# Sampled tokens' output projection and second MLP product from unsplit fp32 operands in two column tiles, with another order of Strassen's products in that block

## The chip, the core and the metric

The kernel runs on one core of a Trainium2 chip. The metric is device time in microseconds of one execution. The engines are named as in the profile: PE (matrix products; PEld is its loading of stationary operands), DVE, ACT, POOL, and SP, which here issues most of the DMA loads.

## The reference

One inference step of a one-layer decoder trunk: 2048 prompt tokens and 64 sampled tokens (8 sequences of 8), width 1024, MLP width 4096, all in fp32. Attention with a forget gate and an mLSTM run beside each other; what concerns the change is the end of the layer, the same for prompt and sampled tokens:

```python
mix = concat([fox_h, mn]) @ w_o                       # output projection, 1024 x 1024
x1  = layer_norm(DN_ALPHA * x + mix, ln1_g, ln1_b)
hid = square(relu(x1 @ w1))                           # first MLP product, 1024 x 4096
y   = layer_norm(DN_ALPHA * x1 + hid @ w2, ln2_g, ln2_b)   # second MLP product, 4096 x 1024
```

## The kernel before

Tokens are cut into 17 tiles: 0 to 15 are 128 prompt tokens each, tile 16 is the 64 sampled tokens. The last phase, `phase_c`, computes the MLP in four blocks of four tiles; the last block (`ci == 3`) has tile 16 as well, so its width `W` is 576 columns instead of 512.

**fp32 through splits.** PE multiplies in fp32r, a faster form that keeps fewer bits. To keep fp32 precision, an operand is split into a high part (ACT copies it to fp32r, `split_hi`, L154) and a low part (DVE subtracts, `split_lo`, L157), and one product becomes three matmuls (`mm3`, L163 to L165). Weights go the same way: `raw()` takes a 512 KB buffer "wr" out of a ring of five (pool `pcw`), SP's queue loads it (in `piece`, L1114), and `piece` splits it into `wh` and `wl` (rings of four). In the kernel before, the raw weights are free again when both splits have read them.

**The MLP in groups.** The 4096 hidden units are done in 16 half-groups of 256: `hidden(p, half)` multiplies the block's tokens by a piece of w1 (two 512 KB loads), and ACT applies relu and square into `hq`. `output(p)` multiplies the hidden units of both halves of group p by w2 with Strassen's seven products in place of eight: for 512 tokens, 512 hidden units and 1024 columns. Each product is 12 matmuls of 512 columns (two token tiles, two steps of 128 hidden units, three of `mm3`) and takes one 512 KB weight: a quarter of w2 (products 1, 2, 3) or a sum of quarters that was prepared in DRAM (`dw2`; products 5, 6, 7, 4). `operands(p)` makes the sums of hidden units on DVE; `s` is the one buffer for them. `add` adds a result to the rows `y` on DVE (L1328), and takes the final norm (`norm_quick`) where a tile's last sum has come in. Products are made ready up to three places ahead (`order[:at_ + 3]`).

**Tile 16's share.** Strassen's products pair up 128-token tiles; tile 16 stands outside. Its hidden units times w2 are plain products, "extras" in the code, with the raw quarters of w2, which are those of products 1, 5, 3 and 2: six `mm3` matmuls of 512 columns with 64 tokens stationary behind each of these four products, from splits `hsh`, `hsl` of the hidden units. Results go to PSUM tile `ph`, and five adds of 64 x 512 go to `y`.

**The sampled stage.** Tile 16's output projection (`sampled`) runs between the two feature halves of `hidden(7, 1)` in block `ci == 2`: four column chunks of 256, each from two loads of w_o that are split; 96 matmuls of 256 columns in PSUM tile `py`. Then tile 16's first norm is taken and its rows go to DRAM, from where the last block takes them.

**Norm vectors.** `vecs(l)` loads the scale and offset of norm l, broadcast over the partitions, into two buffers of the same ring "wr". `C["gb"]` holds those of the second norm: they are loaded at `p == 7` of each block, in the last block ahead of the third product (`at_ == 2`).

**Order.** Each engine works its instructions in the order written into the program. That order is made when the program is built: a planner goes by its own estimates of when instructions are ready, and the code adds constraints (`issue_after`). So it need not be the order of the source. DMA queues start a load when its buffer is free; a load that waits holds up those behind it in the same queue.

Of the kernel before, what the change touches and what calls it, by code (L numbers as in the profile page):

```python
# [10 lines left out]
F32 = mybir.dt.float32  # L11
F32R = mybir.dt.float32r
I32 = mybir.dt.int32
AF = mybir.ActivationFunctionType
OP = mybir.AluOpType
# [21 lines left out]
ALPHA = 2.0 ** 0.25  # L37
# [15 lines left out]
def body(ctx, tc, I, O, stages):  # L53
# [99 lines left out]
    def split_hi(dst, src, scale=1.0):  # L153
        last["ACT"] = A.activation(dst, src, AF.Copy, scale=scale)  # L154

    def split_lo(dst, src, hi, eng=None):
        r = (eng or V).tensor_tensor(dst, src, hi.bitcast(F32), op=OP.subtract)  # L157
        if eng is None:
            last["DVE"] = r
        return r  # L160

    def mm3(ps, wh, wl, xh, xl, first, stop, shared=False):
        T.matmul(ps, wh, xh, start=first, stop=False, skip_group_check=shared)  # L163
        T.matmul(ps, wh, xl, start=False, stop=False, skip_group_check=shared)  # L164
        last["PE"] = T.matmul(ps, wl, xh, start=False, stop=stop, skip_group_check=shared)  # L165

    def layer_norm(x, np_, g, b, wk, tg, eng=None):
        st = wk.tile([128, 2, 6], F32, name="ln_st")
# [911 lines left out]
    def raw():  # L1080

        return pcw.tile([128, 1024], F32, name="wr", bufs=5)
# [165 lines left out]
    def phase_c():  # L1248
# [10 lines left out]
        def sampled():  # L1259

            gb = vecs(1)
            mx = ph.tile([128, 8, 64], F32, name="mxs", tag="s", bufs=1)
            SY.dma_start(mx, dmv[:, :, S:])
            mh = ph.tile([128, 8, 64], F32R, name="mhs", tag="hh", bufs=3)
            ml = ph.tile([128, 8, 64], F32R, name="mls", tag="hl", bufs=3)
            split_hi(mh, mx)
            split_lo(ml, mx, mh)
            y = row()
            SY.dma_start(y[:64], x_of(16))
            for c in range(4):  # L1270
                ps = ppc.tile([128, 512], F32, name="py", bufs=4)[:64, :256]
                for kg in range(2):
                    wh, wl = piece(wo[kg * 512:kg * 512 + 512, c * 256:c * 256 + 256].rearrange("(k p) c -> p k c", p=128))
                    for k in range(4):
                        mm3(ps, mh[:, kg * 4 + k], ml[:, kg * 4 + k], wh[:, k], wl[:, k], kg + k == 0, kg + k == 4)
                s = slice(c * 256, c * 256 + 256)
                V.scalar_tensor_tensor(y[:64, s], y[:64, s], ALPHA, ps, op0=OP.mult, op1=OP.add)
                if c == 0:
                    st = pc.tile([128, 2, 6], F32, name="ln_s2", bufs=5)
                if c % 2:  # L1280
                    V.bn_stats(st[:64, c // 2], y[:64, c * 256 - 256:c * 256 + 256])
            C["normed"] = norm_quick(y[:64], 64, st, *gb, pc, dx1[S:], SY)
# [11 lines left out]
        for ci, blk in enumerate(CB):  # L1294
# [45 lines left out]
            def operands(p):  # L1340

                f1, f2 = H.pop((p, 0)), H.pop((p, 1))
                a11, a21, a12, a22 = f1[:, :, 0:256], f1[:, :, 256:512], f2[:, :, 0:256], f2[:, :, 256:512]
                s = ph.tile([128, 2, 256], F32, name="s", bufs=1)

                def split(x):
                    h = ph.tile([128, 2, 256], F32R, name="hh", bufs=3)
                    l = ph.tile([128, 2, 256], F32R, name="hl", bufs=3)
                    split_hi(h, x)
                    split_lo(l, x, h)  # L1350
                    return h, l

                def w(src):
                    return piece(src.rearrange("p (k c) -> p k c", k=2))

                v = lambda o, x, y, op: V.tensor_tensor(o, x, y, op=op)

                def made(n):
                    if n == 1:
                        r = split(a11), w(I["w2"][p, 0])  # L1360
                        v(s, a21, a22, OP.subtract)
                        v(a21, a11, a21, OP.subtract)
                        v(a11, s, a11, OP.subtract)
                    elif n == 5:
                        r = split(s), w(dw2[p, 0])
                        v(s, a12, a11, OP.add)
                    else:
                        r = {6: lambda: (split(a11), w(dw2[p, 2])), 3: lambda: (split(s), w(I["w2"][p, 3])),
                             7: lambda: (split(a21), w(dw2[p, 1])), 2: lambda: (split(a12), w(I["w2"][p, 2])),
                             4: lambda: (split(a22), w(dw2[p, 3]))}[n]()  # L1370
                    return r

                hs = []
                if W > 512:
                    for f in (f1, f2):
                        x = f[:, :, 512:576]
                        h = ph.tile([128, 2, 64], F32R, name="hsh", bufs=2)
                        l = ph.tile([128, 2, 64], F32R, name="hsl", bufs=2)
                        split_hi(h, x)
                        split_lo(l, x, h)  # L1380
                        hs.append((h, l))
                return made, hs

            def output(p, ahead, begun=None):
                made, hs, ops = ahead
                if p == 0:
                    for t in blk:
                        ys[t] = row()
                        with tc.issue_after(last["ACT"].ins):
                            A.dma_start(ys[t][:tok_n(t)], dx1[tok_r(t):tok_r(t) + tok_n(t)])  # L1390
                X = [ppc.tile([128, 512], F32, name="py", bufs=4) for _ in range(2)]
                Z = None
                ADD, SUB = OP.add, OP.subtract
                plan = {1: ("X", True, False, 0, 0, ADD), 5: ("Z", True, False, 2, 1, ADD), 6: ("X", False, False, 0, 1, SUB),
                        3: ("Z", False, True, 0, 1, ADD), 7: ("X", False, False, 2, 1, SUB), 2: ("Y", True, True, 0, 0, ADD),
                        4: ("X", False, True, 2, 0, ADD)}
                extra = {1: (0, ((0, ADD), (1, SUB))), 5: (0, ((1, ADD),)), 3: (1, ((1, ADD),)), 2: (1, ((0, ADD),))}
                order = (1, 5, 6, 3, 2, 7, 4) if ci == 3 and p == 7 else (1, 5, 6, 3, 7, 2, 4)
                for at_, n in enumerate(order):
                    kind, first_, last_, r0, half, op = plan[n]  # L1400
                    if p == 7 and at_ == 2 and ci == 3:
                        C["gb"] = vecs(2)
                    for m in order[:at_ + 3]:
                        if m not in ops:
                            ops[m] = made(m)
                    (h, l), (wh, wl) = ops[n]
                    for i in range(2):
                        if kind == "X":
                            ps = X[i]
                        else:  # L1410
                            if i == 0 and first_:
                                Z = [None, None]
                            if first_:
                                Z[i] = ppc.tile([128, 512], F32, name="py", bufs=4)
                            ps = Z[i]
                        c = slice(i * 128, i * 128 + 128)
                        for k in range(2):
                            mm3(ps, h[:, k, c], l[:, k, c], wh[:, k], wl[:, k], first_ and k == 0, last_ and k == 1, True)
                        add(blk[r0 + i], half, ps, op)
                        tick(1.28)  # L1420
                        if begun and at_ < 4:
                            turn(ci + 1, at_, i, begun)
                    if n in extra and hs:
                        e, halves = extra[n]
                        ps = ppc.tile([128, 512], F32, name="ph", tag="ph", bufs=2)[:64]
                        for k in range(2):
                            mm3(ps, hs[e][0][:, k], hs[e][1][:, k], wh[:, k], wl[:, k], k == 0, k == 1)
                        for q, op in halves:
                            add(16, q, ps, op)
                        tick(1.28)  # L1430
                if begun:
                    for hf in range(2):
                        turn(ci + 1, 4, hf, begun)
# [19 lines left out]
            for p in range(8):  # L1453
                pre = []
                if p < 7:
                    hidden(p + 1, 0, lambda: pre.append(ahead(p, 1, 5)))
                else:
                    pre.append(ahead(p, 1))
                if p == 6:
# [451 lines left out]
```

## Time and profile before

| | |
|---|---|
| median of 3 runs | 3283.68 us (3271.96 to 3284.96) |
| profiled execution, its own time | 3288.64 us |
| its span in the profile | 3286.9 us |
| mean granted PE clock | 0.983 |
| PE busy | 3157.8 us, 96% |
| DVE, ACT, POOL busy | 64%, 46%, 28% |
| sampled stage | about 2816 to 2830 us of the span |
| last block | about 2860 us to the end |

Times in the profile are microseconds from the start of the span. A row of a timeline gives start, duration, engine, line, operation, tiles, and in brackets the idle time ahead of it with what ended that. A matmul's duration covers its whole way through the pipeline, so durations overlap, and the step from one start to the next tells what one costs. A row of windows gives the stretch, its length, the busy time of PE, PEld, DVE, ACT and POOL, the granted clock, the DMA share and GB/s.

### The profile page before, as it was taken

How to read it: one execution, taken by the hardware profiler on the slowest of the kernel's cores; microseconds unless marked ns; L12 is line 12 of the kernel's file. 1: busy time of each engine (PE TensorE's matmuls, PEld its weight loads, DVE VectorE, ACT ScalarE, POOL GpSimd, SP SyncE). 2: the span in 40 equal slices, each digit the busy share in tenths (PEclk: the TensorE clock that was granted, in tenths of full speed). 3: DMA queues.
4: the chain of work that ended last, by engine and by line, in shares of the span. 5: the costliest groups of instructions: out<-in, count | busy, mean ns of one | idle time of the engine just before them, and what ended most of it. 6: DMA issues, size and time to landing. Idle time of an engine off the chain costs nothing.

```text
span 3286.9 us, 58040 instructions
## 1 busy us (share of the span) xinstructions
PE 3157.8 (96%) x21681; PEld 2568.5 (78%) x21681; DVE 2099.3 (64%) x5083; ACT 1503.5 (46%) x2965; POOL 905.2 (28%) x974
## 2 busy tenths in 40 slices
PE   8999999898979999999999999999999999899997
PEld 8998998887856666677677777777777777798895
DVE  6957565355368787643466658656585666866658
ACT  3343343333358888622334444344454444444442
POOL 0121232322324333276323323333323121000000
PEclk9999999999989999999999999999999999999998
DMA  5575776766678675487887877878779766643332
GB/s 186 149 223 178 238 227 215 238 223 202 218 226 225 157 197 144 159 297 252 307 298 266 293 256 283 318 259 328 283 273 347 241 216 204 201 165 119 121 104 100
DMA packets 339777, 734.36 MB, mean 223 GB/s; under 512 B 63656, under 2 KB 177704, under 8 KB 338600
## 3 DMA queue, kind: packets, MB, share of 16 engines
q1 hardware_dynamic: 252936, 416.71, 39.8%
q0 software_dynamic: 83520, 304.12, 26.7%
q10 hardware_dynamic: 3040, 9.83, 0.8%
q8 instruction: 171, 2.80, 0.3%
q14 instruction: 110, 0.90, 0.1%
HBM read 677.71 MB, written 86.38 MB: 232 GB/s over the span
## 4 chain that ended last, share of the span: by engine, by line
PE 44%; DVE 3%; DMA 2%; issue 1%; POOL 1%; ACT 1%; another core or an unknown queue 0%; DVEq 0%; POOLq 0%
PE ph L163 7%; PE ph L164 7%; PE ph L165 7%; PE py L163 6%; PE py L165 6%; PE py L164 5%; PE sO L1767 2%; PE sQ L1655 2%; DMA vt<-cache_v,idxV 1%; DVE y L1328 1%; DVE wl L157 1%; DMA kT<-cache_k,idxK 1%; PE sT L1724 1%; POOL kT L1632 0%; DMA xr<-cache_v,idxV 0%
## 5 line engine op out<-in xcount | busy, mean ns | idle before, releaser
L157 DVE TENSOR_TENSOR wl<-wr,wh 128x1024 fp32r<-128x1024 f32 x364 | 443.8, 1222 | 364.3 <-ACT wh L154 338.0
L154 ACT ACTIVATE wh<-wr 128x1024 fp32r<-128x1024 f32 x364 | 383.0, 1055 | 320.0 <-PE ph L164 121.8
L163 PE MATMUL ph<-x1h,wh 128*128 128x512 f32 (+1 forms) x1280 | 454.8, 355 | 0.0
L1632 POOL DMA_INDIRECT kT<-cache_k,idxK x256 | 276.5, 1080 | 647.2 <-PE sQ L1655 580.1
L164 PE MATMUL ph<-x1l,wh 128*128 128x512 f32 (+1 forms) x1280 | 452.8, 354 | 0.2 <-DVE x1l L157 0.2
L165 PE MATMUL ph<-x1h,wl 128*128 128x512 f32 (+1 forms) x1280 | 450.2, 353 | 0.0
L163 PE MATMUL py<-wh,hh 128*128 128x512 f32 x896 | 358.0, 402 | 4.2 <-ACT hh L154 1.6
L164 PE MATMUL py<-wl,hh 128*128 128x512 f32 x896 | 353.3, 394 | 3.5 <-DVE wl L157 3.3
L165 PE MATMUL py<-wh,hl 128*128 128x512 f32 x896 | 350.5, 394 | 1.9 <-DVE hl L157 1.9
L1328 DVE TENSOR_TENSOR y<-y,py 128x512 f32<-128x512 f32 x416 | 281.0, 682 | 72.1 <-PE py L165 54.1
L163 PE MATMUL pm<-xh,whi 128*128 128x256 f32 (+1 forms) x1024 | 302.1, 295 | 1.1 <-issue 1.0
L164 PE MATMUL pm<-xl,whi 128*128 128x256 f32 (+1 forms) x1024 | 298.6, 292 | 2.9 <-issue 2.7
L165 PE MATMUL pm<-xh,wlo 128*128 128x256 f32 (+1 forms) x1024 | 297.1, 290 | 1.9 <-issue 1.8
L163 PEld LDWEIGHTS ph<-x1h,wh 128*128 128x128 f32 x1280 | 240.4, 188 | 41.2 <-issue 9.1
L1743 POOL DMA_INDIRECT vt<-cache_v,idxV x164 | 175.8, 1072 | 349.6 <-PE sO L1767 281.2
L164 PEld LDWEIGHTS ph<-x1l,wh 128*128 128x128 f32 x1280 | 240.5, 188 | 34.1 <-issue 3.7
L165 PEld LDWEIGHTS ph<-x1h,wl 128*128 128x128 f32 x1280 | 240.1, 188 | 33.7 <-issue 3.3
L163 PE MATMUL pm<-whi,xh 128*128 128x256 f32 (+2 forms) x816 | 238.7, 293 | 8.8 <-ACT whi L154 8.3
L164 PE MATMUL pm<-wlo,xh 128*128 128x256 f32 (+2 forms) x816 | 234.0, 287 | 1.3 <-issue 0.7
L165 PE MATMUL pm<-whi,xl 128*128 128x256 f32 (+2 forms) x816 | 233.7, 287 | 0.9 <-issue 0.9
L975 ACT ACTIVATE S<-S,mx 128x512 f32<-128x512 f32 (+2 forms) x320 | 208.6, 656 | 16.7 <-DVE mx L961 15.0
L163 PEld LDWEIGHTS py<-wh,hh 128*128 128x128 f32 x896 | 168.8, 189 | 54.3 <-issue 10.6
(372 smaller groups left out, 6821.8 us busy)
## 6 DMA issues: line engine op xcount, KB each, us to landing
wr<-w SPq DMA_DIRECT2D x224, 512.0 KB
wr<-dw SPq DMA_DIRECT2D x128, 512.0 KB
wra<-w_in SPq DMA_DIRECT2D x104, 512.0 KB
dw<-w POOLq DMA_DIRECT2D x48, 512.0 KB
Rb<-dR SPq DMA_DIRECT2D x128, 128.0 KB
xn<-xp_t SPq DMA_DIRECT2D x16, 512.0 KB
kn<-k_prompt SPq DMA_DIRECT2D x64, 128.0 KB
qn<-dq SPq DMA_DIRECT2D x128, 64.0 KB
```

Of the source, the lines that this page charges most:

```text
L154: last["ACT"] = A.activation(dst, src, AF.Copy, scale=scale)
L157: r = (eng or V).tensor_tensor(dst, src, hi.bitcast(F32), op=OP.subtract)
L163: T.matmul(ps, wh, xh, start=first, stop=False, skip_group_check=shared)
L164: T.matmul(ps, wh, xl, start=False, stop=False, skip_group_check=shared)
L165: last["PE"] = T.matmul(ps, wl, xh, start=False, stop=stop, skip_group_check=shared)
L975: last["ACT"] = A.activation(sp[:, :w], sp[:, :w], AF.Exp, bias=mx[:, 7:8], accum_out=lp[:, k:k + 1])
L1328: V.tensor_tensor(y, y, ps, op=op)
L1632: G.indirect_dma_start(out=piece(n), out_offset=None, in_=ck, in_offset=IO(ap=idxK[:, b, j // 2, j % 2:j % 2 + 1], axis=0))
L1655: r = T.matmul(pq[h4 * 32:h4 * 32 + 32, hg].rearrange("p (k c) -> p k c", k=2), z["qb"][:, hd], kv, start=(db == 0), stop=(db == 1), skip_ ...
L1724: T.transpose(p[:, f], z["U"][u][:, hg, f].rearrange("p k t -> p (k t)"), ident)
L1743: G.indirect_dma_start(out=vt.rearrange("p f c -> p (f c)"), out_offset=None, in_=cv, in_offset=IO(ap=idxV[:, b, (kt % 4) * 4 + kt // 4, f ...
L1767: after_ = T.matmul(po[r:r + 32], z["PT"][:, hg, 2 * f + g, pg].rearrange("p h q -> p (h q)"), vts[f][:, g, hg * 256:(hg + 1) * 256], star ...
```

## The change

A new helper, `two_sides`, multiplies unsplit fp32 operands: two products at a time, one into PSUM partitions 0 to 63, the other into partitions 64 to 127, that is, in two tiles of 64 columns of the PE array.

- In `sampled`, mixed activations and w_o stay unsplit. Each column chunk takes four pairs (one matmul on the first half of the contraction, one on the second), and the two halves of PSUM are added to `y` one after the other. The eight weight splits and the split of `mxs` go; raw weights are read by PE itself.
- In the last block, the products' order becomes 1, 2, 5, 3, 6, 7, 4. Tile 16's extras are taken twice per group: behind product 2 with the raw weights of products 1 and 2, behind product 3 with those of 5 and 3; four fp32 matmuls each. The splits `hsh`, `hsl` go. `w()` hands the raw tile on, so it is kept until the extra has read it.
- In the last group of the last block the norm vectors are loaded ahead of the fifth product (`at_ == 4`), no longer ahead of the third.

```diff
+    def two_sides(ps, sides, first, stop):
+
+        for n, (w, x) in enumerate(sides):
+            last["PE"] = T.matmul(ps[n * 64:n * 64 + 64], w, x, start=first, stop=stop, skip_group_check=True)
...
             mx = ph.tile([128, 8, 64], F32, name="mxs", tag="s", bufs=1)
             SY.dma_start(mx, dmv[:, :, S:])
-            mh = ph.tile([128, 8, 64], F32R, name="mhs", tag="hh", bufs=3)
-            ml = ph.tile([128, 8, 64], F32R, name="mls", tag="hl", bufs=3)
-            split_hi(mh, mx)
-            split_lo(ml, mx, mh)
...
-                ps = ppc.tile([128, 512], F32, name="py", bufs=4)[:64, :256]
+                ps = ppc.tile([128, 512], F32, name="py", bufs=4)[:, :256]
+                w = []
                 for kg in range(2):
-                    wh, wl = piece(wo[kg * 512:kg * 512 + 512, c * 256:c * 256 + 256].rearrange("(k p) c -> p k c", p=128))
-                    for k in range(4):
-                        mm3(ps, mh[:, kg * 4 + k], ml[:, kg * 4 + k], wh[:, k], wl[:, k], kg + k == 0, kg + k == 4)
+                    w.append(raw().rearrange("p (k c) -> p k c", k=4))
+                    SY.dma_start(w[kg], wo[kg * 512:kg * 512 + 512, c * 256:c * 256 + 256].rearrange("(k p) c -> p k c", p=128))
+                for k in range(4):
+                    two_sides(ps, [(mx[:, kg * 4 + k], w[kg][:, k]) for kg in range(2)], k == 0, k == 3)
                 s = slice(c * 256, c * 256 + 256)
-                V.scalar_tensor_tensor(y[:64, s], y[:64, s], ALPHA, ps, op0=OP.mult, op1=OP.add)
+                V.scalar_tensor_tensor(y[:64, s], y[:64, s], ALPHA, ps[:64], op0=OP.mult, op1=OP.add)
+                V.tensor_tensor(y[:64, s], y[:64, s], ps[64:128], op=OP.add)
...
                 def w(src):
-                    return piece(src.rearrange("p (k c) -> p k c", k=2))
+                    wr = raw().rearrange("p (k c) -> p k c", k=2)
+                    SY.dma_start(wr, src.rearrange("p (k c) -> p k c", k=2))
+                    return (*piece(None, wr), wr)
...
-                hs = []
-                if W > 512:
-                    for f in (f1, f2):
-                        x = f[:, :, 512:576]
-                        h = ph.tile([128, 2, 64], F32R, name="hsh", bufs=2)
-                        l = ph.tile([128, 2, 64], F32R, name="hsl", bufs=2)
-                        split_hi(h, x)
-                        split_lo(l, x, h)
-                        hs.append((h, l))
+                hs = [f[:, :, 512:576] for f in (f1, f2)] if W > 512 else []
                 return made, hs
+
+            order = (1, 2, 5, 3, 6, 7, 4) if W > 512 else (1, 5, 6, 3, 7, 2, 4)
...
-                extra = {1: (0, ((0, ADD), (1, SUB))), 5: (0, ((1, ADD),)), 3: (1, ((1, ADD),)), 2: (1, ((0, ADD),))}
-                order = (1, 5, 6, 3, 2, 7, 4) if ci == 3 and p == 7 else (1, 5, 6, 3, 7, 2, 4)
+                extra = {2: (1, ((0, 0, ADD), (0, 1, SUB), (1, 0, ADD))), 3: (5, ((0, 1, ADD), (1, 1, ADD)))}
                 for at_, n in enumerate(order):
                     kind, first_, last_, r0, half, op = plan[n]
-                    if p == 7 and at_ == 2 and ci == 3:
+                    if p == 7 and at_ == 4 and ci == 3:
                         C["gb"] = vecs(2)
...
-                    (h, l), (wh, wl) = ops[n]
+                    (h, l), (wh, wl, wr) = ops[n]
...
                     if n in extra and hs:
-                        e, halves = extra[n]
-                        ps = ppc.tile([128, 512], F32, name="ph", tag="ph", bufs=2)[:64]
+                        e, parts = extra[n]
+                        ps = ppc.tile([128, 512], F32, name="ph", tag="ph", bufs=2)
+                        w = ops[e][1][2], wr
                         for k in range(2):
-                            mm3(ps, hs[e][0][:, k], hs[e][1][:, k], wh[:, k], wl[:, k], k == 0, k == 1)
-                        for q, op in halves:
-                            add(16, q, ps, op)
+                            two_sides(ps, [(hs[i][:, k], w[i][:, k]) for i in range(2)], k == 0, k == 1)
+                        for i, q, op in parts:
+                            add(16, q, ps[i * 64:i * 64 + 64], op)
...
-                    hidden(p + 1, 0, lambda: pre.append(ahead(p, 1, 5)))
+                    hidden(p + 1, 0, lambda: pre.append(ahead(p, *order[:2])))
```

## The prediction

> **What bounds the kernel now.** I read the page first (the span, the engines, the chain that ended last), then the busy time by windows over the last 480 us, where the change lies, then the waits of PE and of SP's queue there, and last the records of single operations.
>
> ```profile
> span 3286.9 us, 58040 instructions
> ...
> PE 3157.8 (96%) x21681; PEld 2568.5 (78%) x21681; DVE 2099.3 (64%) x5083; ACT 1503.5 (46%) x2965; POOL 905.2 (28%) x974
> ...
> PE 44%; DVE 3%; DMA 2%; issue 1%; POOL 1%; ACT 1%; another core or an unknown queue 0%; DVEq 0%; POOLq 0%
> ```
>
> PE is busy for 96% and carries 44% of the chain that ended last, against 3% for DVE and 2% for DMA. The last block repeats one piece of work per group of hidden units:
>
> ```profile
> 3003.80 12.84 SPq L1114 DMA_DIRECT2D wr<-w  x5
> 3053.88 12.84 SPq L1114 DMA_DIRECT2D wr<-w  x5
> ...
> 3003.80:3053.88 50.08, 50.08 (x302) 44.43 (x301) 31.99 (x44) 22.66 (x37) 0.00 (x0) 1.00 0.37 116
> ...
> PE px L1143 <- DVE x1l L157: 1.9, 1, 1.9
> ...
> SPq L1114 <- DVE wl L157: 57.7, 12, 12.1
> ```
>
> The first two rows are SP's queue, 50.08 us apart. The third gives busy time of PE, PEld, DVE, ACT and POOL in that stretch, then the granted clock, DMA share and GB/s: PE 50.08 of 50.08 at clock 1.00, DMA 0.37. The fourth is PE's only wait from 2860 to 3250 us; the fifth says that SP waits for buffers, up to 12.1 us at a time: it loads as early as the ring of five "wr" slots lets it. So in the last block only PE's work counts, as long as loads keep this lead.
>
> **The change part by part: the extras.** Per group, the 64 sampled tokens now take 24 fp32r matmuls of 512 columns.
>
> ```profile
> 2904.22 0.40 PE L163 MATMUL ph<-wh,hsh 128*64 128x512 f32 x1
> ...
> 2905.38 0.39 PE L165 MATMUL ph<-wh,hsl 128*64 128x512 f32 x1
> 2905.61 0.39 PE L163 MATMUL py<-wh,hh 128*128 128x512 f32 x1
> 2905.83 0.39 PE L164 MATMUL py<-wl,hh 128*128 128x512 f32 x1
> ...
> L163 PE MATMUL ph<-wh,hsh x64: 389/394/445, 2904.2 to 3250.8; 128*64 128x512 f32 x64
> ```
>
> Six start between 2904.22 and 2905.61, 1.39 us, 0.232 each; 24 are 5.56. (The 389 ns of a record is its pipelined length; the step counts.) The main products step by about 0.227. The nearest row to the new unsplit fp32 matmuls in two column tiles is this attention product:
>
> ```profile
> 1301.72 0.60 PE L988 MATMUL pt<-ident,S 128*128 128x128 f32 x4
> 1302.25 1.08 PE L997 MATMUL po<-PT,vn 128*64 128x256 f32 x8
> 1303.26 0.50 PE L947 MATMUL pS<-ks,qh 128*128 128x512 f32 x1
> ...
> L997 PEld LDWEIGHTS po<-PT,vn x1152: 132/137/231, 934.1 to 1366.9; 128*64 128x64 f32 x192
> ```
>
> It holds two pairs of 256 columns (four matmuls, eight records) in 1.01 us, from 1302.25 to 1303.26. A pair of 256 columns thus costs at most 0.505; I estimate 0.455 (four fp32r passes at half the 0.227 step) and 0.1 for each change between tiled and full array. A pair of 512 columns is then 0.91. The eight weight loads of 132 to 137 ns, about 1.1 us, leave no trace in the 1.01: they lie beside the matmuls. The Trainium skill, "TensorE: Matmul & The Clock Gate", Part 3, The mechanism, says instead that a weight load overlaps matmuls in flight only when its row group differs; column tiles share the row group, so by that rule loads would come on top. It speaks against this change; the row speaks against the rule here, and it is kept as a rival.
>
> Eight matmuls are four pairs, but in the built order the first matmul of the second extra (weights of product 5) stands alone right behind the first extra, and the other three come behind product 5, one of them without a partner. That makes five slots of 0.91, 4.55, and four changes, 0.4: 4.95 for 5.56, −0.6 per group. The adds on DVE stay five. Four splits go:
>
> ```profile
> L154 ACT ACTIVATE hsh<-hq x16: 312/312/314, 2878.6 to 3241.6; 128x128 fp32r<-128x128 f32 x16
> ...
> L157 DVE TENSOR_TENSOR hsl<-hq,hsh x16: 274/282/291, 2881.0 to 3243.2; 128x128 fp32r<-128x128 f32 x16
> ```
>
> That is 0.62 us of ACT and 0.56 of DVE per group, engines at 22.66 and 31.99 of 50.08: worth nothing. The order of products changes no count of matmuls or adds; it acts only through the loads.
>
> **The ring.** Two things take slots. Raw weights of products 1, 2, 5 and 3 are held until PE's extra has read them, where before DVE's split released them. And tile 16's last norm is now reached behind the fourth product of the last group (place 3), while the new norm vectors are loaded at place 4; so it uses the g2 and b2 of the block before, and these two tiles, which lie in "wr" slots, live through the whole last block. A ring of three is left. Per group the queue is then: loads 1, 2, 5; load 3 behind PE's last read of 1; load 6 behind that of 2; 7 and 4 behind the second extra; and the next hidden step's first w1 piece in the slot of 6, once DVE has split that. The prices:
>
> ```profile
> 2821.60 0.37 SPq L1114 DMA_DIRECT2D wr<-w_o  x1
> 2824.80 1.07 ACT L154 ACTIVATE wh<-wr 128x1024 fp32r<-128x1024 f32 x1 [1.44 <-DMA wr<-w_o]
> ...
> 3032.00:3032.50 0.50, 0.50 (x6) 0.50 (x5) 0.00 (x0) 0.00 (x0) 0.00 (x0) 1.00 1.00 401
> ...
> L154 ACT ACTIVATE wh<-wr x364: 1038/1059/1067, 1368.7 to 3253.8; 128x1024 fp32r<-128x1024 f32 x182
> L157 DVE TENSOR_TENSOR wl<-wr,wh x364: 1187/1223/1308, 1370.7 to 3256.4; 128x1024 fp32r<-128x1024 f32 x182
> ...
> 2838.51 0.68 DVE L1328 TENSOR_TENSOR y<-y,py 128x512 f32<-128x512 f32 x1
> 2839.11 0.68 DVE L157 TENSOR_TENSOR x1l<-px,x1h 128x512 fp32r<-128x512 f32 x1
> ```
>
> A load issued at 2821.60 ends ACT's wait at 2824.80: 3.2 us from issue to use. 512 KB at 401 GB/s occupy the engines for 1.3. Splits are 1.06 on ACT, 1.22 on DVE; another DVE step is 0.60. From the first extra's end (t = 0): load 3 lands at about 3.4, wh at 4.5, its wl at 5.9 with a little queueing; DVE does hl (0.6), an add (0.6) and wl of 6 (1.22), 8.4; the w1 piece lands 3.3 to 3.5 later, 11.8; wh at 12.9 to 13.1. PE meanwhile has the lone matmul 0.91, product 5 (12 × 0.227 = 2.73), two more slots 1.82, three changes 0.3, and products 3 and 6 (5.46): 11.2. Then the hidden step's matmuls stand ahead of product 7 in PE's queue and need that wh: a wait of 1.7 to 1.9, with product 7's matmuls behind it. I take 1.9. Bounds: 0 (loads and splits 15% quicker) to 3.2 (one whole load late, as nothing more is serial). A group gets −0.6 + 1.9 = +1.3; seven groups, 9. With the bounds, −4 to +18.
>
> **The sampled stage** (output projection of tile 16, in block three).
>
> ```profile
> 2816.17 0.36 PE L163 MATMUL py<-wh,mhs 128*64 128x256 f32 x1
> ...
> 2828.37 0.28 PE L165 MATMUL py<-wh,mls 128*64 128x256 f32 x1
> ...
> 2829.80 0.73 PE L163 MATMUL py<-wh,hh 128*128 128x512 f32 x2 [1.15 <-ACT wh L154]
> ...
> 2836.90 0.50 PE L164 MATMUL py<-wl,hh 128*128 128x512 f32 x1 [2.82 <-DVE wl L157]
> ...
> PE py L164 <- DVE wl L157: 4.0, 3, 2.8
> ...
> 2838.12:2841.53 3.41, 3.41 (x10) 2.69 (x9) 3.41 (x6) 1.19 (x2) 0.00 (x0) 0.56 0.93 315
> ```
>
> It lasts 13.6 us, 2816.17 to 2829.80. After: 16 pairs × 0.455 = 7.3 and some transposes between (about 0.4). But g1 and b1 hold two slots there, and each pair reads both weights of its column chunk: three slots, eight loads, so the second weight of chunks 2, 3 and 4 is issued only when PE has finished the chunk before, and lands 3.2 later. Three such waits, the first shortened by about 1: 8.6. Sum 16.3, +2.7. The loads of the last group's products queue behind these, in the slots PE frees, where DVE's splits freed them before; they delay the next products by 1 to 3 us, I take 2.5. Bounds of the stage: −6 (no wait: 7.7) to +8. PE's clock: the wait of 2.82 was followed by a stretch of 3.41 us at clock 0.56, which costs 1.5. Waits of 3.2 can do so again, the 1.9 in the block's row did not show it; I add 2, from 0 to 4. The Trainium skill, same page, What's actually happening, puts the trigger at an idle window of about 3.4 us, free-running; by it none of the single waits need halve the clock, and the sum would lose this 2. The 2.82 row differs from it. The eight ACT and DVE splits that go lay beside the matmuls and waits.
>
> **The last group and the tail.**
>
> ```profile
> 3262.12 0.39 PE L163 MATMUL py<-wh,hh 128*128 128x512 f32 x1
> ...
> 3281.98 1.40 DVE L192 SCALAR_TENSOR_TENSOR y<-y,ln_r,b 128x512 f32<-128x512 f32 x2
> ```
>
> Some 20 us of DVE norms follow the last products. No hidden step stands in this group, so its load waits come ahead of products, at most 3.2 for one; but tile 16's norm moves ahead, which takes up to 3 us (its four half-row steps) out of the tail. The new order also ends with 6, 7, 4 instead of 2, 7, 4. I take +1, from −3 to +5.
>
> **Sum:** 2.7 + 2.5 + 2 (stage) + 9 + 1 = +17, on the profiled execution 3288.6 → 3306. That execution lies 5 us above the median of 3283.7, so the median goes to about 3301.
>
> **Rivals.** *Waits hidden* (no change): the ring of three exists, but loads and splits keep just ahead of PE, as 1.9 us of slack in a chain of 13 would do. Then −0.6 × 8 and the stage's +7: +2, 3286. For it: the DMA share of 0.37; against: every link of the chain is serial.
>
> *Every load in time* (faster): PE's own work decides. It turns on whether loads land before PE asks for them, in the stage as well; the lone matmul then overlaps a neighbour or costs nothing beside it. Extras 3.64 + 0.4 for 5.56, −1.5 × 8 = −12; stage 7.7 for 13.6, −6: −18, 3266. For it: PE is 50.08 of 50.08 busy, so each us of work saved shows if loads keep up. Against: the slots counted above.
>
> *Column tiles in series* (slower still): pairs don't overlap, or the loads come on top. In series the extras are 8 × 0.91 + 0.4 = 7.7, +2.1 per group, and the stall shrinks to about 0.9 as PE reaches it one slot later: +3 × 7 = 21; the stage's matmuls 14.6 for 7.3, partly beside its loads, and the tail: about +34, 3318. Against: the 1.01 us row. By the page's rule alone, 16 loads × 0.134 = 2.1 per group would give nearly the same.
>
> **How the numbers follow.** A measurement of this kernel can tell about 0.5%, 16 us, from no change: 3267 to 3300 counts as the same. The forecast (ring of three, a stall per group) has 0.62; its own range is 3288 to 3314 and its middle lies at the bound, 0.43 above and 0.19 within. Waits hidden 0.17, all within. Every load in time 0.09, faster. Series 0.12, slower. So faster 0.09, same 0.36, slower 0.55. The range 3282 to 3320 leaves out the faster case and the upper half of the series case, about 0.15, and the ends of the unknown costs.
>
> **What would show it.** In the profile after: PE waits of 1.5 to 2 us in the last block, once per group, before a "ph" matmul of the hidden step and released by ACT's wh; SP's period near 51.4 instead of 50.08; "wr" loads of products 3 and 6 issued only behind PE's first extra; an extra of two pairs in 1.82. In the sampled stage, three PE waits near 3 us released by w_o loads, in 16 us altogether. If the period is 49.5 or less, the ring argument is wrong; if a pair of 512 columns takes 1.8, the pairing is.

## The result and the profile after

The changed kernel is slower by about 1%: ratio of its runs to those of the kernel before 1.0102, 95% interval 1.0081 to 1.0122; medians 3312.2 against 3278.1 us, 8 runs each. That is +34 us, twice the +17 of the prediction, on the predicted side and inside its range.

The profiled execution took 3302.1 us, ten less than the median; here are its span, its engines and its chain:

```profile
span 3300.4 us, 57753 instructions
...
PE 3150.9 (95%) x21585; PEld 2542.1 (77%) x21585; DVE 2101.5 (64%) x5062; ACT 1488.8 (45%) x2940; POOL 903.1 (27%) x974
...
PE 10%; DVE 2%; DMA 1%; issue 0%; ACT 0%; DVEq 0%; ACTq 0%; SPq 0%
```

The chain could be followed back over 13% of the span only, so the page doesn't say what bounds the rest. PE is busy for 6.9 us less, and yet the span is 13.5 longer. The full lengthening isn't even in this pair of spans: the last hidden step of block three is reached at 2776.1 us before and 2758.2 after. Up to there the change touches nothing and PE does the same number of matmuls, but this execution had 68.3 us at half clock for 92.2, which is about 12 of the 17.9. So the stretches around the change are compared. The windows go from the last hidden step of block three to the first relu of block four (with the sampled stage), then one group of block four, two in the kernel after; columns are length, PE, PEld, DVE, ACT, POOL, granted clock, DMA share, GB/s. Before:

```profile
2776.07:2866.65 90.58, 81.28 (x456) 65.19 (x455) 72.01 (x108) 44.22 (x57) 4.24 (x4) 0.98 0.63 202
2889.77:2939.84 50.07, 50.07 (x302) 44.42 (x301) 32.09 (x43) 22.42 (x37) 0.00 (x0) 1.00 0.48 165
```

After:

```profile
2758.17:2859.42 101.25, 85.68 (x424) 62.88 (x423) 65.10 (x105) 35.62 (x48) 4.24 (x4) 0.88 0.54 182
2882.54:2934.51 51.97, 49.92 (x294) 42.12 (x293) 32.32 (x41) 21.95 (x35) 0.00 (x0) 1.00 0.48 157
2934.51:2988.82 54.31, 51.57 (x294) 43.26 (x293) 32.42 (x41) 22.07 (x36) 0.00 (x0) 0.97 0.33 107
```

The first stretch is 10.7 us longer, though it holds 32 matmul records fewer, at clock 0.88 in place of 0.98. A group is 1.9 longer where the clock stayed at 1.00 and 4.2 longer where it fell to 0.97. Over all seven groups it is 21.0, and from the last relu to the end −0.4: together +31.4, which agrees with the medians' +34.

PE's waits in the last block and in the stage, and the largest wait of SP's queue in the last block:

```profile
PE ph L163 <- ACT wh L154: 15.6, 7, 2.7
...
PE py L170 <- DMA wr<-w_o: 7.5, 3, 2.7
...
SPq L1359 <- PE ph L170: 184.5, 17, 19.5
```

Seven waits, one per group, each ahead of a hidden step's "ph" matmul and ended by ACT's wh; three waits for w_o in the stage. The queue's loads now wait longest for PE's extras (L170), where before the change they waited for DVE's splits. One group in PE's and SP's timelines:

```profile
2899.81 2.79 PE L170 MATMUL ph<-wr,hq 128*64 128x512 f32 x10
2902.53 0.50 PE L163 MATMUL py<-wh,hh 128*128 128x512 f32 x1
...
2905.49 1.93 PE L170 MATMUL ph<-wr,hq 128*64 128x512 f32 x6
2907.35 1.21 PE L163 MATMUL py<-wh,hh 128*128 128x512 f32 x4
...
2915.14 0.40 PE L163 MATMUL ph<-x1h,wh 128*128 128x288 f32 x1 [2.05 <-ACT wh L154]
```

```profile
2901.77 0.33 SPq L1359 DMA_DIRECT2D wr<-w  x1
2902.20 5.75 SPq L1359 DMA_DIRECT2D wr<-dw  x3
2909.91 8.17 SPq L1119 DMA_DIRECT2D wr<-w  x4
```

Two records are one fp32 matmul. Ten records in 2.72 us are two pairs and the lone matmul, six in 1.86 are the other three: slots of 0.91, if coming and going are spread over them. Load 3 is issued at 2901.77, when the first extra's second pair has ended; the next w1 piece at 2909.91; its wh ends PE's wait at 2915.14.

**The clock.** Where the granted clock falls, it does so for whole windows of 3.41 us on a fixed grid. Two pairs of neighbouring windows of the kernel after:

```profile
2913.86:2917.27 3.41, 2.13 (x11) 1.87 (x12) 3.41 (x5) 1.67 (x2) 0.00 (x0) 1.00 0.73 199
2917.27:2920.68 3.41, 3.41 (x24) 3.18 (x23) 3.14 (x5) 1.51 (x2) 0.00 (x0) 1.00 0.79 252
2965.06:2968.47 3.41, 0.67 (x5) 0.62 (x5) 3.41 (x6) 1.69 (x3) 0.00 (x0) 1.00 0.60 195
2968.47:2971.88 3.41, 3.41 (x10) 2.64 (x9) 1.86 (x3) 1.06 (x1) 0.00 (x0) 0.50 0.70 211
```

In the first pair a wait of 2.05 us is split by the grid: 1.28 idle in this window, the next at full clock. In the second pair a wait of 2.74 lies wholly in one window, PE is busy for 0.67 of it, and the next window runs at half clock: 10 matmul records in place of 24. From the last hidden step of block three to the last of block four the profile shows 34.1 us at half clock after, 3.4 before.

### The profile page after: what moved, and what is told of

It reads as the page before. It is cut to its first block, busy times and chain, and to the rows that moved or that the text cites. A ratio compares the mean times of both kernels' runs of the same rounds, so it can differ in the third digit from the quotient of the medians.

```text
span 3300.4 us, 57753 instructions
## 1 busy us (share of the span) xinstructions
PE 3150.9 (95%) x21585; PEld 2542.1 (77%) x21585; DVE 2101.5 (64%) x5062; ACT 1488.8 (45%) x2940; POOL 903.1 (27%) x974
## 5 line engine op out<-in xcount | busy, mean ns | idle before, releaser
L157 DVE TENSOR_TENSOR wl<-wr,wh 128x1024 fp32r<-128x1024 f32 x356 | 434.4, 1222 | 299.2 <-ACT wh L154 291.2
L154 ACT ACTIVATE wh<-wr 128x1024 fp32r<-128x1024 f32 x356 | 374.7, 1054 | 408.9 <-PE ph L164 157.1
L163 PE MATMUL ph<-x1h,wh 128*128 128x512 f32 (+1 forms) x1280 | 456.1, 357 | 15.7 <-ACT wh L154 15.6
L165 PEld LDWEIGHTS ph<-x1h,wl 128*128 128x128 f32 x1280 | 241.1, 189 | 34.1 <-issue 3.3
L163 PEld LDWEIGHTS py<-wh,hh 128*128 128x128 f32 x896 | 169.3, 191 | 68.6 <-issue 14.7
```

## The experiments

All are compared with the kernel before on the same chip. The theories: A, the two slots held by old norm vectors leave a ring of three, and that makes the wait per group; B, not the ring, but the raw weights held for PE, or the new order; C, idle PE time halves the clock, and that is the rest; D, the 64-column fp32 matmuls themselves lower it.

**Free the two slots.** In the changed kernel the norm vectors are loaded ahead of tile 16's last norm:

```diff
-                    if p == 7 and at_ == 4 and ci == 3:
+                    if p == 7 and at_ == 2 and ci == 3:
```

> The changed kernel, with the norm vectors of the last block loaded ahead of the third product of its last group (as before the change) in place of the fifth. Tile 16's last norm then uses the new vectors, the old ones are freed at the block's start, and five slots are left for weights. Theory A (two held slots make the ring of three, and that makes the wait per group): PE's seven waits for the hidden step's wh, 15.6 us in all, go to under 2; the period per group falls from 52 to 54 us to 49.5 to 50.0; half-clock windows in the groups go from 3 to 0; time 3283 to 3290 against 3278 before, since the sampled stage's cost stays. Rival B (the waits come from raw weights held until the extras have read them, or from the new order): waits of 1.5 us or more per group stay, time 3302 or more.

Measured: 3280.9 us, ratio 0.9995 (0.9977 to 1.0014): one line takes back the whole loss. A group:

```profile
2901.01:2949.80 48.79, 48.69 (x294) 42.24 (x293) 31.95 (x41) 21.89 (x36) 0.00 (x0) 1.00 0.49 168
...
2918.29 3.65 PE L170 MATMUL ph<-wr,hq 128*64 128x512 f32 x16
```

No wait for wh is left, no half clock in the groups, and the period is 48.8, better than the expected 49.5. The second row says why: the planner now puts all eight fp32 matmuls in one run of sixteen records, four full pairs in 3.65 us, and PE goes over to the tiled array and back once instead of twice. With three slots load 3 had to wait for the first extra's readings, so the extras stood apart.

**Hold the slots, keep the split extras.** In the kernel before, the vectors are loaded too late for tile 16's norm:

```diff
-                    if p == 7 and at_ == 2 and ci == 3:
+                    if p == 7 and at_ == 5 and ci == 3:
```

> The kernel before, with only the load of the last block's norm vectors moved behind tile 16's last norm (sixth place), so that the old vectors hold two of the five slots through the last block; extras, order and stage are those of before. Theory A in its strong form (three slots alone are too few): PE waits in most groups, period 51 or more, time 3285 to 3295. Weaker form (three slots hurt only together with raw weights that are held until PE has read them): period 50.1 to 50.6, time 3278 to 3283. Rival B expects no change at all: 50.1 and 3278.

Measured: 3279.0, ratio 0.9992 (0.9978 to 1.0007), groups of 50.1, one of which is:

```profile
2934.42:2984.50 50.08, 50.08 (x302) 44.44 (x301) 31.98 (x43) 22.61 (x38) 0.00 (x0) 1.00 0.38 116
```

Three slots alone cost nothing; A's strong form is wrong.

**The same with the new order.** The kernel before, with order 1, 2, 5, 3, 6, 7, 4 and held vectors, still with split extras:

```diff
-                order = (1, 5, 6, 3, 2, 7, 4) if ci == 3 and p == 7 else (1, 5, 6, 3, 7, 2, 4)
+                order = (1, 2, 5, 3, 6, 7, 4) if ci == 3 else (1, 5, 6, 3, 7, 2, 4)
...
-                    if p == 7 and at_ == 2 and ci == 3:
+                    if p == 7 and at_ == 4 and ci == 3:
...
-                    hidden(p + 1, 0, lambda: pre.append(ahead(p, 1, 5)))
+                    hidden(p + 1, 0, lambda: pre.append(ahead(p, 1, 2 if ci == 3 else 5)))
```

> The kernel before with the new order of products (1, 2, 5, 3, 6, 7, 4) in its last block and the old norm vectors held there as in the change (three slots), but with the split extras behind products 1, 2, 5 and 3, so that raw weights are free once they are split; stage of before. With three slots, e2_held_vectors in the old order lost nothing. If raw weights held until PE has read them are what turns three slots into a wait: no waits, period 50.1 to 50.6, time 3279. If the new order does it: waits of 1.5 us or more per group, period 51.5 or more, 3290 or more.

Measured: ratio 0.9994 (0.9977 to 1.0011), groups of 50.1, no wait:

```profile
2932.46:2982.53 50.07, 50.07 (x302) 44.40 (x301) 32.30 (x43) 22.75 (x38) 0.00 (x0) 1.00 0.38 116
```

So neither the order nor three slots make the wait, and not the held raw weights with five slots either; it takes three slots and raw weights that are held until PE has read them.

**One slot held.** As the first experiment, but tile 16's norm takes the old scale and the new offset:

```diff
+                        g_old = C["gb"][0]
                         C["gb"] = vecs(2)
+                        C["gb16"] = g_old, C["gb"][1]
```

> e1_fresh_vectors, but tile 16's last norm takes the old scale g2 and the new offset b2, so that one of the five slots is held through the last block: a ring of four. By the chain of the prediction a fourth slot lets load 3 start before the first extra ends, about 3 us earlier, which is more than the wait of 2.2 us: period 48.8 to 49.3, time 3281, as with five. If the wait is in proportion to held slots: half of it stays, period 50 or more, 3290 or more.

Measured: ratio 1.0027 (1.001 to 1.0044). A group, and all waits of PE in the seven groups:

```profile
2936.77:2986.62 49.85, 49.22 (x294) 42.05 (x293) 32.13 (x41) 21.94 (x36) 0.00 (x0) 1.00 0.37 117
...
PE py L163 <- DVE y L1332: 1.7, 5, 0.4
PE py L163 <- ACT hh L154: 1.5, 2, 1.0
PE py L163 <- ACT wh L154: 0.8, 4, 0.3
```

Between the two expectations: no half clock in the groups, idle PE time of 0.5 to 1.3 us per group (5.0 in seven), PE's busy time 0.5 more than with five slots. As the chain had it, a fourth slot takes away the hidden step's wait for wh. But short waits of the products come up in its place, for DVE's adds and for splits, so a group is 1.1 us longer than with five slots; why they come up wasn't tested.

**The sampled stage by itself**, once left out of the change and once alone:

```diff
 # the changed kernel, with sampled() of the kernel before
+                    wh, wl = piece(wo[kg * 512:kg * 512 + 512, c * 256:c * 256 + 256]...)
+                        mm3(ps, mh[:, kg * 4 + k], ml[:, kg * 4 + k], wh[:, k], wl[:, k], ...)
 # the kernel before, with two_sides and sampled() of the changed kernel
+                    two_sides(ps, [(mx[:, kg * 4 + k], w[kg][:, k]) for kg in range(2)], k == 0, k == 3)
```

> The changed kernel with the sampled stage of the kernel before (split operands). From the trace of after, the stretch from the last hidden step of block three to the first of block four was 10.7 us longer than before, with 20.5 us more at half clock. If that is the new stage's doing: time 3312 - 11 = 3301, one half-clock window in the stretch as before. If the half clock came from somewhere else (other state of the chip): no more than 4 us less, 3308.

> The kernel before with the new sampled stage alone; the last block is that of before. By the same reading: 3278 + 11 = 3289, with three waits of about 2.5 us for w_o loads and 4 to 7 half-clock windows in the stage; last block's period 50.1. If the stage costs only its waits (+3 without the clock): 3281.

Measured: 1.0064 (1.0041 to 1.0086), +21 us, for the groups without the stage, from four runs; 1.0026 (1.0007 to 1.0046), +8.5, for the stage alone. The sum, 0.9%, agrees with the change's 1.0% within the intervals. How many windows of the groups run at half clock varies: five in the trace without the new stage, three in that of the change. The stretch around the new stage, in the kernel with the stage alone, has the low clock again (27.3 us at half clock, more than expected) and is 11.9 us longer than before in this trace:

```profile
2763.80:2866.31 102.51, 85.95 (x424) 62.30 (x423) 65.08 (x105) 35.63 (x49) 4.24 (x4) 0.87 0.54 179
```

**Fill the waits with work.** To the first experiment's kernel, where the groups have no half clock:

```diff
+                if c < 3:
+                    z = ppc.tile([128, 512], F32, name="pf", tag="ph", bufs=2)
+                    xh = C["x"][0]
+                    with tc.issue_after(last["PE"].ins):
+                        for j in range(14):
+                            last["PE"] = T.matmul(z, xh[:, 0, 0:128], xh[:, 1, 0:512], start=j == 0, stop=j == 13)
```

> e1_fresh_vectors with work added: behind each of the first three column chunks of the sampled stage PE does 14 full-array fp32r matmuls of 512 columns into a scratch PSUM tile that nobody reads, 3.2 us each time at full clock, about as long as the waits for w_o loads there. Theory C (idle PE time within a window of 3.41 us halves the clock of the next): with the waits filled, half-clock time in the stretch around the stage falls from 23.9 us to under 8, and the stretch from 101.6 us to 92 to 97, though 42 matmuls more are done; time 3272 to 3278. Rival D (the 64-column fp32 matmuls themselves lower the clock, or the chip was in another state): half clock stays near 20 us or more, and the stretch becomes longer, 104 us or more, 3284 or more.

Measured: 3277.4 us, ratio 0.9991 (0.9974 to 1.0008). The stretch, of the first experiment and then of this one:

```profile
2776.28:2877.91 101.63, 86.94 (x424) 63.79 (x423) 65.89 (x107) 35.51 (x49) 4.55 (x5) 0.88 0.55 183
```

```profile
2764.69:2864.19 99.50, 90.42 (x466) 67.70 (x465) 62.76 (x98) 34.45 (x48) 3.69 (x3) 0.95 0.56 185
...
PE py L170 <- DMA mxs<-dmix: 4.3, 1, 4.3
```

42 matmuls more, 9.6 us of work at full clock, and the stretch is 2.1 us shorter: half-clock time fell from 23.9 to 10.2 us, PE's idle time from 14.7 to 9.1. The three waits for w_o are gone; a new one, 4.3 us for the stage's activations, is followed by a window at half clock, and a wait of 3.1 us for DVE's x1l by two more, so the hoped-for 92 to 97 us weren't reached. The sum closes: +9.6 of work, −5.6 of waits, −6.2 of clock (half of the 12.4 us less of half-clock time in which PE worked), −2.2 against −2.1 measured. D is refuted: the same 64-column matmuls ran, and the clock rose; and in the first experiment's groups they run at clock 1.00 throughout. The kernels' total times don't tell the two apart (the intervals overlap); the windows do.

**Five slots for the stage.** The first norm's vectors are loaded behind the w_o loads:

```diff
-            gb = vecs(1)
             mx = ph.tile([128, 8, 64], F32, name="mxs", tag="s", bufs=1)
...
+            gb = vecs(1)
             C["normed"] = norm_quick(y[:64], 64, st, *gb, pc, dx1[S:], SY)
```

> e1_fresh_vectors with the first norm's vectors in the sampled stage loaded behind the w_o loads instead of ahead of them, so that w_o has five slots in place of three. If the three waits for w_o are of the ring, as in the groups: they go from 6.6 us to under 3, half-clock time in the stretch from 23.9 to 10 or less, the stretch from 101.6 to 91 to 95, time 3270 to 3275; the norm may now wait for its vectors, off PE's path. If the loads are limited by the DMA queues and not by slots: the waits stay at 5 us or more, and time at 3280.

Measured: 3265.2, ratio 0.9952 (0.9931 to 0.9972). This kernel is faster than before and after.

```profile
2768.87:2857.12 88.25, 80.26 (x424) 60.17 (x423) 61.76 (x98) 34.54 (x47) 3.69 (x3) 0.94 0.61 205
...
PE py L163 <- ACT wh L154: 5.2, 1, 5.2
PE py L170 <- DMA wr<-w_o: 2.1, 2, 1.3
```

The stretch is 88.3 us for 101.6, and 90.6 in the kernel before. The waits for w_o went from 6.6 to 2.1 us, as the ring would have it, and half clock to 10.2; part of the wait was passed on to the next product's first wh (5.2 us).

**The old stage with five slots.** The first experiment with the split stage of the kernel before; the edit is that of the stage experiment above.

> e1_fresh_vectors with the split sampled stage of the kernel before: only the last block's extras and order are those of the change, with five slots. The groups in e1_fresh_vectors took 48.8 us for 50.07 before, seven times, and the stretch around the stage was 11 us longer than before. If the two parts add: 3281 - 9 = 3272, against 3281 before, ratio 0.997. If the stage's cost was made up elsewhere: 3279 or more.

Measured: 3266.3, ratio 0.9963 (0.9944 to 0.9982). The parts add; the extras and the order, with five slots, are worth about 12 us by the medians' ratio, 9 by the groups' lengths.

**The extras in one column tile.** The first experiment's kernel, with both sides of the extras in partitions 0 to 63, each in a PSUM tile of its own:

```diff
-                        for k in range(2):
-                            two_sides(ps, [(hs[i][:, k], w[i][:, k]) for i in range(2)], k == 0, k == 1)
+                        pt = [ps[:64], ppc.tile([128, 512], F32, name="ph", tag="ph", bufs=2)[:64]]
+                        for i in range(2):
+                            for k in range(2):
+                                last["PE"] = T.matmul(pt[i], hs[i][:, k], w[i][:, k], start=k == 0, stop=k == 1)
```

> e1_fresh_vectors with the extras' eight fp32 matmuls all in the first 64 columns of the array, each side in a PSUM tile of its own, so that none can run beside another. If column tiles run in pairs: eight matmuls take 7.3 us for 3.65, a group 52.4 us for 48.8, time about +29, 3310. If the pairs had not overlapped: no change, 48.8 and 3281.

Measured: ratio 1.0084 (1.0061 to 1.0108); a group:

```profile
2945.93:2998.49 52.56, 52.46 (x294) 43.04 (x293) 32.13 (x41) 21.66 (x35) 0.00 (x0) 1.00 0.34 111
```

3.8 us more per group, against 3.65 for four more slots: column tiles do run in pairs, and the rival of tiles in series is refuted.

## Why the prediction was right, and where its size was off

*The ring of three*: right, and shown by taking it away. The prediction named two things that take slots; the experiments show that it needs both: three slots cost nothing without the held raw weights, and these cost no wait with five slots. The chain held nearly link by link. From the first extra's end (2901.6) the prediction had wl of 6 done at 8.4; the w1 load was issued at 8.3. It had PE at the hidden step at 11.2; PE got there at 11.3. Only the last load was slower: 4.1 us to use, not 3.3 to 3.5; three loads were issued right behind it, but whether that is the reason wasn't tested. So the wait was 2.05 here and 2.2 on the mean, for a forecast of 1.9.

*−0.6 of PE work per group*: too favourable. In groups without half clock PE's busy time fell by 0.15 (49.92 for 50.07), and over the seven together it rose by 0.3 (21.0 less 15.6 of waits and 5.1 of clock). The extras themselves cost what was said, but by two errors that cancel. The weight loads of the first extra show its steps, and the second main matmul behind it starts late:

```profile
2900.29 0.14 PEld L170 LDWEIGHTS ph<-wr,hq 128*64 128x64 f32 x2 [0.29 <-issue]
2900.72 0.14 PEld L170 LDWEIGHTS ph<-wr,hq 128*64 128x64 f32 x2 [0.29 <-issue]
2901.15 0.14 PEld L170 LDWEIGHTS ph<-wr,hq 128*64 128x64 f32 x1 [0.29 <-issue]
...
2902.53 0.50 PE L163 MATMUL py<-wh,hh 128*128 128x512 f32 x1
...
2902.86 0.39 PE L164 MATMUL py<-wl,hh 128*128 128x512 f32 x1
```

A step is 0.43, and a pair, two steps, 0.86 rather than 0.91. Coming and going take 0.35 us per extra rather than 0.2, with the slow first step of 0.33 behind it. Both extras together are 4.98 for the 4.95 of the prediction. The saving was lost elsewhere, for the most part in two places: the other steps between main products, worked out from their starts, rose from 0.2277 to 0.2291; and the last matmul ahead of a wait counts with its whole length, 0.39, where one without a wait counts with its step of 0.23. What makes the main steps longer is open.

*The stage*: waits of 7.5 for 8.6. The stage itself, from its first matmul to the next product's:

```profile
2798.45:2819.17 20.72, 12.88 (x70) 6.50 (x69) 3.49 (x8) 2.92 (x5) 0.00 (x0) 0.67 0.53 177
```

PE worked for 8.6 us of it at half clock; less half of that it is 16.4, for the 16.3 of the prediction. Without the clock the whole stretch is 3.0 us longer (10.7 less half of the 15.4 us of added half-clock time in which PE worked), where the prediction had 2.7 + 2.5 = 5.2. So the 2.5 for the delay of later loads was too much.

*The clock*: this is the term that was mis-sized most. The prediction gave 2 us, in the stage alone, and none for the groups, because the one wait of 1.9 in the block's row hadn't halved the clock. Half-clock time grew by 30.7 us: in the stage by 20.5, where PE stood idle for 5.0 of it, so it cost 7.7; in the groups by three windows, 10.2 us, behind waits of 2.3 to 2.7 us, which cost 5.1. Together 12.8 where 2 was said. With 15.9 for the groups, 3.0 for the stage and −0.4 for the tail, 12.8 makes up the +31.4. The spread of the changed kernel's runs, 3294 to 3319 us, goes with it: the fastest has a mean clock of 0.984, the two slowest 0.978.

So the sum of +17 fell short by 14: by 10.8 in the clock and by 6.8 in the groups (15.9 for 9.1: 2.3 of waits, 4.5 of PE's work), while stage and tail came out 3.6 lower than said. The mechanism and the side were right; that the time lies inside the range is in part luck, since the bounds for the wait and the loads, which made it wide enough, had no half clock of the groups in them.

*The two rules weighed.* The Trainium skill, "TensorE: Matmul & The Clock Gate", What's actually happening, has the clock halve after an idle window of about 3.4 us. The grid and the length agree with the windows here. That the whole window must be idle does not: a wait of 2.74 us in a window with 0.67 of PE work sufficed. The Trainium skill, same page, Part 3, The mechanism, has weight loads overlap with matmuls in flight only for different row groups. Here that doesn't hold: the loads begin with the steps of 0.43, last 0.14, and sixteen records with their loads ran in 3.65 us, so the column tiles' loads were hidden.

*Rivals*: waits hidden, refuted by the seven waits. Column tiles in series, refuted by the slots of 0.91 and by the run with one column tile. Every load in time (−18, 3266) is not what the change did. With the slots freed in both places, for the last block and for the stage, 3265 came out for 3279 before, but not by the rival's parts: the groups gave 9.2 us for its 12 and the stretch around the stage 2.3 for its 6. That the run with the old stage came out at 3266 too is a coincidence.

## What to carry to other kernels

A buffer that is read by one more engine, later, lengthens its hold, and what else lies in the same ring decides whether that shows: list every tile that shares the ring, with its last reader, before counting slots. A short wait of PE costs more than its length when it takes more than about half of a window of the clock's grid, so a wait of 2 to 3 us is to be priced with the half-clock window behind it (up to 1.7 us if PE works through it), times the share of times that it falls into one window. Even matmuls whose result nobody reads cost nothing in such waits here: 0.9991 with them, 0.9995 without.

## What the runs showed of the hardware

The clock's threshold: in the twelve traces of this case, from 1400 to 3250 us of the span, on the grid of 3.41 us, windows at full clock with PE idle for less than 1.2 us were never followed by half clock (6,240 of them); with 1.2 to 1.6 us, 1 of 53 was; with 1.6 to 2.0, 21 of 36; with 2.0 or more, all 68. Idle time is the gaps between matmuls that the trace records, so the edge, near half of the window, is soft.

A pair of unsplit fp32 matmuls with 64 stationary columns each and 512 moving ones takes 0.86 us from start to start in two column tiles, or 0.91 by the length of a run of four pairs (sixteen records in 3.65); one alone takes as long. In one column tile the same eight matmuls took 3.8 us more.
